# mLSTM denominators once per head and stream, and row scaling on ScalarE, in a two-layer encoder trunk

## The chip, the cores and the metric

The kernel runs on one core of a Trainium2 chip. The metric is the device time of one execution in microseconds, lower is better; the time of a kernel is the median of its runs. The engines are TensorE (PE; PEld is its weight load), VectorE (DVE), ScalarE (ACT), GpSimd (POOL) and SyncE (SP), which issues nearly all DMAs. Each engine runs its own instructions in order.

## The reference, cut to what matters

A hybrid encoder trunk of two layers (model width 1024) is applied to two request groups, a prompt of 256 tokens and a sample of 512 tokens. In each layer, eight grouped-query attention heads (C), four mLSTM heads (B) and four dilated attention heads (A) work on one projected input; cross-attention and a gated MLP follow. The mLSTM part, per head and chunk, in both directions:

```python
num = w_state[..., None] * jnp.einsum('nhld,nhde->nhle', qc, C) + jnp.einsum('nhls,nhse->nhle', w_intra, vc)
den = w_state * jnp.einsum('nhld,nhd->nhl', qc, n) + jnp.sum(w_intra, axis=-1)
h = num / jnp.maximum(jnp.abs(den), jnp.exp(-m_loc))[..., None]
...
hs = (hcat[:B] + flip(hcat[B:])).transpose(0, 2, 1, 3)
```

The forward and the backward scan each have their own denominator for each token; the two results are added.

## The kernel before, in words

The tokens of both groups stand side by side, 768 columns; `STREAMS` are (256, 512), the sample, and (0, 256), the prompt. The kernel does the mLSTM as masked attention over the whole stream. A query tile is 128 tokens, so a head has 4 tiles in the long stream and 2 in the short one, 6 per head, 24 per layer and 48 in all.

`attend` does one head and stream: for each query tile the scores (L375, L376, into one of two PSUM banks "S"), then `soft`, which turns scores into weights `p`; then the transposes of all tiles' weights (L387, into one of two banks "T"), a split into a high and a low half (ACT cast L183, DVE subtract L158), and the products with the values (L395, L396, into the single bank "Y").

For mLSTM heads `soft` is `b_soft`. For one tile it adds the triangular masks to the gate rows of the diagonal block (DVE, L158, with `cs`), takes Exps of the gate rows (ACT, L755 to L759: forward weights left of and on the diagonal, backward weights on and right of it), and multiplies them by the scores with a sum (DVE, L761, shown in the trace as CUSTOM_DVE_ANT_0 and a DVE_READ_ACCUMULATOR2): `p[:, 0:d1]` is the forward part with sum 0, `wb = gd[:, 1]` the backward diagonal block with sum 1, `p[:, d1:n]` the rest of the backward part with sum 2. L761 is the last reader of the scores, so it gives the bank "S" back. Then, per tile, four small DVE steps on the [128, 4] tile `dn` (add, absolute value, maximum with a column of `colm`, reciprocal), the row multiplies `smul("V", ...)` (L172, one on the forward part, and one on the backward rest if there is one), and a scalar_tensor_tensor (STT, L161) that adds the scaled backward diagonal block to `p`.

The weights and the gate tiles `gdt` lie in `arena_f`, of 13,824 fp32 columns, which is handed out by the `Arena` class in the order of the program text, oldest free place first. Gate rows come by DMA from `scr_g` (L725).

The order on each engine is set by a scheduler from priorities. `ahead(first, second)` gives `first` a lower priority, so that the projections of the next group of heads fill the gaps of the heads at hand: `b_proj(1)` beside `b_attn(0)` (heads 0 and 1), `a_proj(0)` beside `b_attn(1)` (heads 2 and 3). The heads themselves follow one another as the buffers permit.

Of the kernel before, what the change touches and what calls it, by code (L numbers as in the profile page):

```python
# [9 lines left out]
F32 = mybir.dt.float32  # L10
# [3 lines left out]
ALU = mybir.AluOpType  # L14
# [94 lines left out]
def trunk_kernel(ctx, tc, xT, memT, w_in, w_out, w_xq, w_xkv, w_xo, w_up, w_dn, w_dnt, par, fin_g, cst, fmk, tabs,  # L109
# [251 lines left out]
        for p0, src in pieces:  # L361
            SY.dma_start(out=dst.bitcast(F32)[p0:p0 + src.shape[0], :src.shape[1]], in_=src)

    def attend(qs, q0, nq, KH, KL, k0, nk, vv, vt0, e, y, y0, soft):
        n = nq * 128
        ni = 512 // nk
        ptiles, held = [], []
        for b in range(nq // ni):
            s = bank("S", "s").rearrange("p (i k) -> p i k", i=ni)
            pt = palloc()  # L370
            p = pt.rearrange("p (i k) -> p i k", i=ni)
            for j in range(ni):
                i = b * ni + j
                qa = qs[:, q0 + i * 128:q0 + (i + 1) * 128]
                PE.matmul(s[:, j], qa, KH[:, k0:k0 + nk], start=True, stop=False)  # L375
                PE.matmul(s[:, j], qa, KL[:, k0:k0 + nk], start=False, stop=True)  # L376
            soft(s, p, b * ni, ni)
            ptiles += [p[:, j] for j in range(ni)]
            held.append(pt)
        yps = bank("Y", "yps")  # L380
        nkt = nk // 128
        nb = 512 // n
        for kb in range(0, nkt, nb):
            t = bank("T", "t")
            for j in range(nb):
                for i in range(nq):
                    PE.transpose(t[:, j * n + i * 128:j * n + (i + 1) * 128],  # L387
                                 ptiles[i][:, (kb + j) * 128:(kb + j + 1) * 128], ident)
            ph, pl = asm.tile(512), asm.tile(512)
            hi_op(pick("ph_" + SITE[0], "A"), ph, t)  # L390
            tt(pl, t, ph.bitcast(F32), ALU.subtract)
            for j in range(nb):
                kt = kb + j
                w = vv[:, vt0 + kt]
                PE.matmul(yps[:, :n], w, ph[:, j * n:(j + 1) * n], start=kt == 0, stop=False)  # L395
                PE.matmul(yps[:, :n], w, pl[:, j * n:(j + 1) * n], start=False, stop=kt == nkt - 1)  # L396
            asm.free(ph, pl)
        af.free(*held)
        yo = y[64 * e:64 * e + 64, y0:y0 + n]
        hi_op(pick("yo_" + SITE[0], "A"), yo, yps[64 - 64 * e:128 - 64 * e, :n])  # L400
        tt(yo, yps[64 * e:64 * e + 64, :n], yo, ALU.add)
# [111 lines left out]
    def mixers(l, xt, x_dram, stats):  # L513
# [215 lines left out]
        def b_attn(pb, sv):  # L729
            SITE[0] = "b%d" % pb  # L730
            sts, vv, rows = sv
            for e in range(2):
                qs, K = sts[e]
                hd = 2 * pb + e
                for c0, n in STREAMS:
                    gb = rows[e][:, 2 * c0:2 * c0 + 2 * n].rearrange("p (d k) -> p d k", d=2)
                    attend(qs, c0, n // 128, K[:, :T], K[:, T:], c0, n, tok(vv[e]), c0 // 128, e, yt[5 + pb], c0,
                           b_soft(gb, c0, n, hd))
                af.free(rows[e])
                ar.free(qs, K, vv[e])  # L740

        def b_soft(gb, c0, n, hd):
            def soft(s, p, i0, ni):
                for j in range(ni):
                    one(s[:, j], p[:, j], i0 + j)

            def one(s, p, i):
                ti = c0 // 128 + i
                d0, d1 = i * 128, (i + 1) * 128
                nm = lambda d: colm[:, 2 * ti, d, hd:hd + 1]  # L750
                gdt = af.tile(256)
                gd = gdt.rearrange("p (d k) -> p d k", d=2)
                tt(gd, gb[:, :, d0:d1], tri, ALU.add)
                if i:
# [2 lines left out]
                A.activation(gd[:, 1], gd[:, 1], ACT.Exp, bias=nm(1))  # L757
                if d1 < n:
                    A.activation(p[:, d1:n], gb[:, 1, d1:n], ACT.Exp, bias=nm(1))  # L759
                dn = st.tile([128, 4], F32, tag="dn", name="dn")  # L760
                ttr = lambda o, s0, s1, c: V.tensor_tensor_reduce(  # L761
                    out=o, in0=s[:, s0:s1], in1=o, scale=0.125, scalar=0.0,
                    op0=ALU.mult, op1=ALU.add, accum_out=dn[:, c:c + 1])
                wb = gd[:, 1]
                ttr(p[:, 0:d1], 0, d1, 0)
                ttr(wb, d0, d1, 1)
                if d1 < n:
                    ttr(p[:, d1:n], d1, n, 2)
                    tt(dn[:, 1:2], dn[:, 1:2], dn[:, 2:3], ALU.add)
                stt(dn[:, 0:2], dn[:, 0:2], -1.0, dn[:, 0:2], ALU.mult, ALU.max)  # L770
                tt(dn[:, 0:2], dn[:, 0:2], colm[:, 2 * ti + 1, :, hd], ALU.max)
                V.reciprocal(dn[:, 0:2], dn[:, 0:2])
                smul("V", p[:, 0:d1], p[:, 0:d1], dn[:, 0:1])
                stt(p[:, d0:d1], wb, dn[:, 1:2], p[:, d0:d1], ALU.mult, ALU.add)
                if d1 < n:
                    smul("V", p[:, d1:n], p[:, d1:n], dn[:, 1:2])
                af.free(gdt)
            return soft

        def a_proj(pg):  # L780
            if pg == 0:
# [593 lines left out]
```

## Time and profile before

| What | Value |
|---|---|
| median of 3 runs | 2203.67 us (2197.82 to 2207.76) |
| profiled execution, its own time | 2199.17 us |
| its span from the first to the last instruction | 2197.3 us |
| mean granted TensorE clock | 0.952 of full speed |
| instructions | 31315 |

The span is the profiled execution from its first to its last instruction, on the one core. The busy share of an engine is an average over stages with different limits; what the mLSTM heads of the two layers cost is read from their own stretches, between about 250 and 345 us and between about 1328 and 1426 us.

### The profile page before, as it was taken

The page shows a single profiled execution, that of the slowest core. Times are in us where ns is not written, and L with a number is a line of the kernel's source. Part 1 is how long each engine was busy: PE and PEld are TensorE (multiplying, and loading weights), DVE is VectorE, ACT ScalarE, POOL GpSimd, SP SyncE. Part 2 cuts the span into 40 slices and gives each one's busy share as a digit, 9 for nine tenths or more (in the row PEclk, how much of TensorE's full clock was granted, in tenths as well). Part 3 has the DMA queues.
Part 4 walks back from the last instruction along what each step waited for, and adds up shares of the span by engine and source line. Part 5 has one row for each costly group of instructions (what it writes and reads, how often), then busy time and mean ns, then how long its engine had stood idle before and what let it go on. Part 6 is the DMA issues. An engine that isn't in the chain of part 4 may idle for free.

```text
span 2197.3 us, 31315 instructions
## 1 busy us (share of the span) xinstructions
PE 2032.2 (92%) x11256; PEld 1801.6 (82%) x11256; DVE 1924.4 (88%) x4191; ACT 1032.9 (47%) x2030; POOL 2.3 (0%) x28
## 2 busy tenths in 40 slices
PE   7989888998889999999999897899978999999996
PEld 5868677787779999999888685787868899999995
DVE  8777897877899999999978879888888999999997
ACT  4256645546533333333443666474654333333342
POOL 0000000000000000000000000000000000000000
PEclk8989989999899999999999898899988999999998
DMA  5523334343212222222234234344421222222211
GB/s 178 147 72 91 92 94 100 97 125 106 77 59 86 68 68 68 68 69 75 92 140 121 72 80 114 76 124 131 129 77 63 82 68 68 68 67 68 74 33 68
DMA packets 64684, 195.16 MB, mean 89 GB/s; under 512 B 8264, under 2 KB 11592, under 8 KB 63760
## 3 DMA queue, kind: packets, MB, share of 16 engines
q1 hardware_dynamic: 64528, 193.15, 30.1%
q8 instruction: 89, 1.46, 0.3%
q14 instruction: 67, 0.55, 0.1%
HBM read 150.17 MB, written 10.71 MB: 73 GB/s over the span
## 4 chain that ended last, share of the span: by engine, by line
PE 70%; DVE 21%; ACT 4%; DMA 3%; issue 2%; SPq 1%; DVEq 0%; ACTq 0%
PE rps L1075 8%; PE rps L1073 8%; PE rps L1074 8%; DVE arena_f L158 5%; PE rps L1116 5%; PE rps L1117 5%; PE rps L1118 5%; PE prS L213 4%; PE prS L214 4%; PE prS L215 4%; DVE arena_r L158 3%; DVE arena_f L161 2%; DVE xall L158 2%; PE t L387 2%; DVE wl L158 2%
## 5 line engine op out<-in xcount | busy, mean ns | idle before, releaser
L183 ACT CAST wh<-arena_f 128x512 fp32r<-128x512 f32 x280 | 170.6, 620 | 267.2 <-PE rps L1074 216.5
L183 ACT CAST wh<-wr 128x512 fp32r<-128x512 f32 x268 | 164.7, 620 | 264.4 <-PE rps L1074 101.8
L158 DVE TENSOR_TENSOR arena_f<-arena_f 128x512 f32<-128x512 f32 (+3 forms) x381 | 271.9, 732 | 16.3 <-DMA arena_f<-in_w_up 6.4
L158 DVE TENSOR_TENSOR wl<-wr,wh 128x512 fp32r<-128x512 f32 x288 | 197.1, 687 | 35.0 <-ACT wh L183 30.9
L1075 PE MATMUL rps<-xha,wl 128*128 128x384 f32 x640 | 212.1, 338 | 8.4 <-DVE wl L158 8.4
L1073 PE MATMUL rps<-xha,wh 128*128 128x384 f32 x640 | 216.3, 338 | 1.6 <-ACT wh L183 1.5
L1074 PE MATMUL rps<-xla,wh 128*128 128x384 f32 x640 | 216.0, 338 | 0.0
L158 DVE TENSOR_TENSOR xall<-rps,xall 128x256 f32<-128x256 f32 (+1 forms) x384 | 198.8, 554 | 15.9 <-PE rps L1196 5.1
L1116 PE MATMUL rps<-arena_r,wh 128*128 128x512 f32 (+1 forms) x608 | 202.6, 340 | 3.3 <-DVE xall L158 3.3
L1117 PE MATMUL rps<-arena_r,wh 128*128 128x512 f32 (+1 forms) x608 | 200.9, 338 | 0.5 <-DVE arena_r L158 0.4
L213 PE MATMUL prS<-xha,wh 128*128 128x512 f32 x480 | 193.6, 407 | 5.4 <-DVE arena_r L158 3.3
L215 PE MATMUL prS<-xha,wl 128*128 128x512 f32 x480 | 193.5, 404 | 3.3 <-DVE wl L158 3.1
L214 PE MATMUL prS<-xla,wh 128*128 128x512 f32 x480 | 193.0, 404 | 0.8 <-DVE xla L158 0.8
L158 DVE TENSOR_TENSOR wl<-arena_f,wh 128x512 fp32r<-128x512 f32 x280 | 189.6, 687 | 1.2 <-ACT wh L183 1.0
L158 DVE TENSOR_TENSOR arena_f<-rps,arena_f 128x384 f32<-128x384 f32 x280 | 151.9, 555 | 33.5 <-PE rps L1075 29.8
L1118 PE MATMUL rps<-arena_r,wl 128*128 128x512 f32 (+1 forms) x608 | 178.1, 338 | 0.0
L1073 PE MATMUL rps<-arena_r,wh 128*128 128x384 f32 x480 | 162.8, 340 | 1.3 <-ACT wh L183 1.3
L1074 PE MATMUL rps<-arena_r,wh 128*128 128x384 f32 x480 | 161.8, 337 | 0.0
L1075 PE MATMUL rps<-arena_r,wl 128*128 128x384 f32 x480 | 156.0, 339 | 0.6 <-DVE wl L158 0.5
L158 DVE TENSOR_TENSOR arena_r<-t,arena_r 128x512 fp32r<-128x512 f32 x184 | 125.1, 685 | 27.3 <-ACT arena_r L183 26.6
L213 PE MATMUL prP<-xha,wh 128*128 128x256 f32 x480 | 141.9, 296 | 7.0 <-DVE arena_f L158 3.4
L387 PE MATMUL t<-cs,arena_f 128*128 128x128 f32 x736 | 128.0, 291 | 13.6 <-DVE arena_r L158 8.3
(211 smaller groups left out, 4976.8 us busy)
## 6 DMA issues: line engine op xcount, KB each, us to landing
arena_f<-in_w_up SPq DMA_DIRECT2D x80, 512.0 KB
wr<-in_w_in SPq DMA_DIRECT2D x42, 512.0 KB
wr<-in_w_dn SPq DMA_DIRECT2D x40, 512.0 KB
wr<-in_w_out SPq DMA_DIRECT2D x32, 512.0 KB
arena_r<-arena_r SPq DMA_DIRECT2D x32, 384.0 KB
arena_r<-arena_r SPq DMA_DIRECT2D x48, 192.0 KB
xall<-in_xT SPq DMA_DIRECT2D x8, 768.0 KB
arena_r<-arena_r SPq DMA_DIRECT2D x64, 96.0 KB
```

Of the source, the lines that this page charges most:

```text
L158: V.tensor_tensor(out, a, b, op=op)
L183: A.copy(out, a)
L213: PE.matmul(ps, h[:, j], xh[i][:, c0:c0 + n], start=i == 0, stop=False)
L214: PE.matmul(ps, h[:, j], xl[i][:, c0:c0 + n], start=False, stop=False)
L215: PE.matmul(ps, lo[:, j], xh[i][:, c0:c0 + n], start=False, stop=i == tot - 1)
L387: PE.transpose(t[:, j * n + i * 128:j * n + (i + 1) * 128], ptiles[i][:, (kb + j) * 128:(kb + j + 1) * 128], ident)
L1073: PE.matmul(ps, h[:, k], x[k], start=k == 0, stop=False)
L1074: PE.matmul(ps, h[:, k], x[4 + k], start=False, stop=False)
L1075: PE.matmul(ps, lo[:, k], x[k], start=False, stop=k == 3)
L1116: PE.matmul(ps, h[:, m], hh[i][:, c], start=k == 0 and not tail, stop=False)
L1117: PE.matmul(ps, h[:, m], hlo[i][:, c], start=False, stop=False)
L1118: PE.matmul(ps, lo[:, m], hh[i][:, c], start=False, stop=i == b - 1)
```

## The change

The four small steps are no longer done per tile. `dn` becomes a [128, 4, 3] tile per head and stream (four buffers of the pool), the reductions of each tile write their row of it, and after the last tile of the stream a new function `settle_p` does the add, the absolute value, the maximum and the reciprocal once, on all tiles. It then scales the rows of each tile with `smul("A", ...)`, an ACT activation Copy with a scale from a column (L170), both parts of a tile, and adds the scaled backward diagonal block with the STT on DVE as before. The gate tiles are held until then. What is computed is the same.

```diff
-    def attend(qs, q0, nq, KH, KL, k0, nk, vv, vt0, e, y, y0, soft):
+    def attend(qs, q0, nq, KH, KL, k0, nk, vv, vt0, e, y, y0, soft, settle_p=None):
...
+        if settle_p:
+            settle_p(ptiles)
         yps = bank("Y", "yps")
...
         def b_soft(gb, c0, n, hd):
+            nq, t0 = n // 128, c0 // 128
+            dn = st.tile([128, 4, 3], F32, tag="dn", name="dn", bufs=4)
+            gds = []
...
-                dn = st.tile([128, 4], F32, tag="dn", name="dn")
                 ttr = lambda o, s0, s1, c: V.tensor_tensor_reduce(
                     out=o, in0=s[:, s0:s1], in1=o, scale=0.125, scalar=0.0,
-                    op0=ALU.mult, op1=ALU.add, accum_out=dn[:, c:c + 1])
-                wb = gd[:, 1]
+                    op0=ALU.mult, op1=ALU.add, accum_out=dn[:, i, c:c + 1])
                 ttr(p[:, 0:d1], 0, d1, 0)
-                ttr(wb, d0, d1, 1)
+                ttr(gd[:, 1], d0, d1, 1)
                 if d1 < n:
                     ttr(p[:, d1:n], d1, n, 2)
-                    tt(dn[:, 1:2], dn[:, 1:2], dn[:, 2:3], ALU.add)
-                stt(dn[:, 0:2], dn[:, 0:2], -1.0, dn[:, 0:2], ALU.mult, ALU.max)
-                tt(dn[:, 0:2], dn[:, 0:2], colm[:, 2 * ti + 1, :, hd], ALU.max)
-                V.reciprocal(dn[:, 0:2], dn[:, 0:2])
-                smul("V", p[:, 0:d1], p[:, 0:d1], dn[:, 0:1])
-                stt(p[:, d0:d1], wb, dn[:, 1:2], p[:, d0:d1], ALU.mult, ALU.add)
-                if d1 < n:
-                    smul("V", p[:, d1:n], p[:, d1:n], dn[:, 1:2])
-                af.free(gdt)
-            return soft
+
+            def settle_p(ps):
+                tt(dn[:, 0:nq - 1, 1], dn[:, 0:nq - 1, 1], dn[:, 0:nq - 1, 2], ALU.add)
+                d = dn[:, 0:nq, 0:2]
+                stt(d, d, -1.0, d, ALU.mult, ALU.max)
+                tt(d, d, colm[:, 2 * t0 + 1:2 * (t0 + nq):2, :, hd], ALU.max)
+                V.reciprocal(d, d)
+                for i, p in enumerate(ps):
+                    d0, d1 = i * 128, (i + 1) * 128
+                    smul("A", p[:, 0:d1], p[:, 0:d1], dn[:, i, 0:1])
+                    if d1 < n:
+                        smul("A", p[:, d1:n], p[:, d1:n], dn[:, i, 1:2])
+                    stt(p[:, d0:d1], gds[i][:, 128:256], dn[:, i, 1:2], p[:, d0:d1], ALU.mult, ALU.add)
+                af.free(*gds)
+            return soft, settle_p
```

The scheduler plans the order anew. The place shown is in the first layer, the end of head 0 (long and short stream); the names carry the numbers of their tiles. On DVE the order before is this: `dn_2413`, `dn_2431` and their like are tiles of single query tiles, L172 the row multiplies, L161 on `arena_f_76` the STTs.

```order
L172 TENSOR_SCALAR arena_f_76<-arena_f_76,dn_2431 128x512
L172 TENSOR_SCALAR arena_f_76<-arena_f_76,dn_2413 128x384
L172 TENSOR_SCALAR arena_f_76<-arena_f_76,dn_2413 128x128
L158 TENSOR_TENSOR xall_70<-yps_2118,xall_70 64x256
L161 SCALAR_TENSOR_TENSOR arena_f_76<-arena_f_76,dn_2394 128x128
L158 TENSOR_TENSOR dn_2569<-dn_2569 128x1
L161 SCALAR_TENSOR_TENSOR dn_2550<-dn_2550 128x2
L158 TENSOR_TENSOR dn_2531<-dn_2531,colm_466 128x2
L772 RECIPROCAL dn_2487<-dn_2487 128x2
L172 TENSOR_SCALAR arena_f_76<-arena_f_76,dn_2502 128x256
L161 SCALAR_TENSOR_TENSOR arena_f_76<-arena_f_76,dn_2431 128x128
```

In the change the same engine has this there; `dn_2368` is the tile of head 0's long stream, `dn_2464` that of its short stream, `dn_2506` that of head 1's long stream, and the additions with `cs_84` are masks for later tiles.

```order
L158 TENSOR_TENSOR dn_2464<-dn_2464,colm_466 128x2x2
L158 TENSOR_TENSOR xall_70<-yps_2118,xall_70 64x256
L161 SCALAR_TENSOR_TENSOR arena_f_76<-arena_f_76,dn_2368 128x128
L158 TENSOR_TENSOR dn_2506<-dn_2506 128x3
L779 RECIPROCAL dn_2464<-dn_2464 128x2x2
L158 TENSOR_TENSOR arena_f_76<-arena_f_76,cs_84 128x256 x2
L161 SCALAR_TENSOR_TENSOR arena_f_76<-arena_f_76,dn_2368 128x128
L158 TENSOR_TENSOR arena_f_76<-arena_f_76,cs_84 128x256 x4
L161 SCALAR_TENSOR_TENSOR arena_f_76<-arena_f_76,dn_2368 128x128
L158 TENSOR_TENSOR arena_r_77<-vps_2348,arena_r_77 128x4x64
L161 SCALAR_TENSOR_TENSOR arena_f_76<-arena_f_76,dn_2464 128x128 x2
```

The row multiplies and most small steps are gone from DVE; the four STTs of the long stream stand apart, with additions for later tiles between them. On ACT, at the same place, the order before is this: the copies are the results of the attention heads before (`yps_2068`, `yps_2118`), L347 is a cast of the next group's values, L756 and L757 are Exps of later tiles.

```order
L183 COPY xall_70<-yps_2068 64x512
L757 ACTIVATE arena_f_76<-arena_f_76,colm_466 128x128 x2
L183 COPY xall_70<-yps_2118 64x256
L347 CAST arena_r_77<-vps_2348 128x4x64
L183 CAST arena_r_77<-t_2440 128x512
L183 CAST arena_r_77<-t_2449 128x512
```

In the change ACT has this there, with L762 and L763 in the place of L756 and L757.

```order
L183 COPY xall_70<-yps_2118 64x256
L170 ACTIVATE arena_f_76<-arena_f_76,dn_2368 128x128
L170 ACTIVATE arena_f_76<-arena_f_76,dn_2368 128x384
L170 ACTIVATE arena_f_76<-arena_f_76,dn_2368 128x256 x2
L170 ACTIVATE arena_f_76<-arena_f_76,dn_2368 128x384
L170 ACTIVATE arena_f_76<-arena_f_76,dn_2368 128x128
L170 ACTIVATE arena_f_76<-arena_f_76,dn_2368 128x512
L347 CAST arena_r_77<-vps_2348 128x4x64
L170 ACTIVATE arena_f_76<-arena_f_76,dn_2464 128x128 x2
L170 ACTIVATE arena_f_76<-arena_f_76,dn_2464 128x256
L762 ACTIVATE arena_f_76<-arena_f_76,colm_466 128x128
L763 ACTIVATE arena_f_76<-arena_f_76,colm_466 128x128
```

The ten row multiplies of head 0 stand together, behind the copies, and the Exps of later tiles and the casts of transposed weights come after them.

## Rows read from the trace of the kernel before

**Rows 1.** The page's first part: busy us (share of the span) xinstructions
```profile
PE 2032.2 (92%) x11256; PEld 1801.6 (82%) x11256; DVE 1924.4 (88%) x4191; ACT 1032.9 (47%) x2030; POOL 2.3 (0%) x28
```

**Rows 2.** Busy time by stretch; columns as the first line says
```profile
core 0: us, PE busy (x) PEld busy (x) DVE busy (x) ACT busy (x) POOL busy (x), PEclk, DMA share, GB/s
252.00:288.00 36.00, 25.53 (x92) 17.05 (x91) 35.72 (x165) 23.59 (x63) 0.00 (x0) 0.72 0.38 97
288.00:316.00 28.00, 28.00 (x168) 25.16 (x167) 24.33 (x86) 10.87 (x23) 0.00 (x0) 0.94 0.18 49
316.00:344.00 28.00, 23.57 (x115) 18.18 (x114) 27.64 (x118) 16.81 (x41) 0.00 (x0) 0.88 0.41 100
1330.00:1366.00 36.00, 23.89 (x94) 16.28 (x93) 31.84 (x154) 20.23 (x54) 0.00 (x0) 0.77 0.44 107
1366.00:1398.00 32.00, 32.00 (x189) 28.08 (x190) 25.84 (x77) 13.28 (x28) 0.00 (x0) 0.99 0.27 81
1398.00:1426.00 28.00, 21.39 (x96) 16.13 (x95) 27.61 (x129) 15.54 (x37) 0.00 (x0) 0.76 0.44 104
```

**Rows 3.** Groups by form on DVE: count | busy us, mean ns | idle before
```profile
L161 DVE SCALAR_TENSOR_TENSOR arena_f<-arena_f,dn 128x128 f32<-128x128 f32 x48 | 16.2, 347 | 0.0
...
L172 DVE TENSOR_SCALAR arena_f<-arena_f,dn 128x128 f32<-128x128 f32 x32 | 8.3, 283 | 0.0
L172 DVE TENSOR_SCALAR arena_f<-arena_f,dn 128x256 f32<-128x256 f32 x24 | 7.5, 343 | 0.0
...
L172 DVE TENSOR_SCALAR arena_f<-arena_f,dn 128x384 f32<-128x384 f32 x16 | 6.6, 411 | 0.0
L158 DVE TENSOR_TENSOR dn<-dn 128x1 f32<-128x1 f32 x32 | 4.9, 155 | 0.1
L172 DVE TENSOR_SCALAR arena_f<-arena_f,dn 128x512 f32<-128x512 f32 x8 | 3.8, 476 | 0.0
```

**Rows 4.** The tile `dn`, who waited for it: us in total, times
```profile
  PE s L375: 22.4, 17
```

**Rows 5.** Timeline of DVE, around 271.6 us: start us, length us, instruction
```profile
271.60 0.15 DVE L158 TENSOR_TENSOR dn<-dn 128x1 f32<-128x1 f32 x1
271.67 0.15 DVE L161 SCALAR_TENSOR_TENSOR dn<-dn 128x2 f32<-128x2 f32 x1
271.74 0.15 DVE L158 TENSOR_TENSOR dn<-dn,colm 128x2 f32<-128x2 f32 x1
271.81 0.16 DVE L772 RECIPROCAL dn<-dn 128x2 f32<-128x2 f32 x1
```

**Rows 6.** Groups by form on ACT: count | busy us, mean ns | idle before
```profile
L185 ACT ACTIVATE xha<-xall,pr 128x512 fp32r<-128x512 f32 x42 | 29.1, 717 | 21.3 <-DVE xall L158 15.2 <-PE prS L215 5.9
...
L757 ACT ACTIVATE arena_f<-arena_f,colm 128x128 f32<-128x128 f32 x48 | 18.6, 393 | 4.3 <-DVE arena_f L158 4.3
...
L755 ACT ACTIVATE arena_f<-arena_f,colm 128x384 f32<-128x384 f32 x8 | 4.9, 611 | 1.6 <-DVE arena_f L158 1.1 <-PE t L387 0.5
...
L755 ACT ACTIVATE arena_f<-arena_f,colm 128x256 f32<-128x256 f32 x8 | 4.0, 500 | 3.4 <-DVE arena_f L158 3.4
```

**Rows 7.** Timeline of ACT, around 264 us
```profile
263.63 0.41 ACT L756 ACTIVATE arena_f<-arena_f,colm 128x128 f32<-128x128 f32 x1
263.92 0.41 ACT L757 ACTIVATE arena_f<-arena_f,colm 128x128 f32<-128x128 f32 x1
264.21 0.41 ACT L756 ACTIVATE arena_f<-arena_f,colm 128x128 f32<-128x128 f32 x1
```

**Rows 8.** Busy time by stretch, the two parts of the first one
```profile
252.00:264.00 12.00, 9.14 (x40) 6.00 (x38) 11.91 (x47) 11.84 (x32) 0.00 (x0) 0.86 0.21 50
264.00:288.00 24.00, 16.39 (x52) 11.05 (x53) 23.81 (x119) 11.75 (x33) 0.00 (x0) 0.65 0.47 121
```

**Rows 9.** Waits of ACT in 1326 to 1436 us: total, times, longest
```profile
ACT arena_f L755 <- DMA arena_f<-scr_g: 7.1, 1, 7.1
```

**Rows 10.** The chain that ended last, same stretch: start us, length us
```profile
1344.29 7.73 DMA arena_f<-scr_g
```

More of the change, by code (lines that the diff above doesn't have):

```diff
@@ L737, in b_attn @@
                     attend(qs, c0, n // 128, K[:, :T], K[:, T:], c0, n, tok(vv[e]), c0 // 128, e, yt[5 + pb], c0,
-                           b_soft(gb, c0, n, hd))
+                           *b_soft(gb, c0, n, hd))
                 af.free(rows[e])
@@ L747, in one @@
             def one(s, p, i):
-                ti = c0 // 128 + i
                 d0, d1 = i * 128, (i + 1) * 128
-                nm = lambda d: colm[:, 2 * ti, d, hd:hd + 1]
+                nm = lambda d: colm[:, 2 * (t0 + i), d, hd:hd + 1]
                 gdt = af.tile(256)
+                gds.append(gdt)
                 gd = gdt.rearrange("p (d k) -> p d k", d=2)
```

## The prediction

> **What bounds the kernel now.** I began with the page's first part, which gives each engine's busy time. TensorE is busy for 92% of the 2197.3 us span and VectorE (DVE) for 88%, while ScalarE (ACT) is busy for 47% [rows 1]. The average says that TensorE is the bound, but the change touches only the mLSTM heads, so the second view was busy time by stretch. It shows four stretches in which DVE is the full engine and TensorE is not: 252 to 288 and 1330 to 1366 us (the first two heads of each layer), 316 to 344 and 1398 to 1426 us (the other two) [rows 2]. DVE is busy 35.72 of 36 us, 27.64 of 28, 31.84 of 36 and 27.61 of 28. TensorE is idle for 10.5, 4.4, 12.1 and 6.6 us of them, 33.6 us in all, and its mean granted clock is 0.72 to 0.88. In the stretches between (288 to 316, 1366 to 1398) TensorE is busy throughout with projections. So time can be had only inside the four stretches, and the idle 33.6 us is about as much as there is, if the clock stays as it is.
>
> The third view, everything that touches the denominator tile `dn`, says who waits: the score matmuls on TensorE (L375) waited 17 times, 22.4 us together, for DVE work on `dn`, that is for the two score banks that the reductions of L761 give back [rows 4]. DVE's pace frees the banks; TensorE follows.
>
> **What the change removes from DVE.** Two kinds of work leave. First the 80 row multiplies of L172, which go to ACT. Their mean durations at 128, 256, 384 and 512 columns are 283, 343, 411 and 476 ns, times 32, 24, 16 and 8: 26.2 us [rows 3]. Second the four small steps (add, abs, max, reciprocal). They are 32 + 48 + 48 + 48 = 176 instructions, and become 16 of each, one set per head and stream (four heads, two streams, two layers): 64, so 112 fewer. Each lasts 0.15 to 0.16 us, but in the timeline they start 0.07 us apart (271.60, 271.67, 271.74, 271.81) [rows 5]: on a full engine only the distance of starts counts. 112 x 0.07 = 7.8 us. The same overlap of 0.08 us, taken off each of the 80 multiplies, leaves 26.2 - 6.4 = 19.8 us. DVE is relieved of 27.6 us, 6.9 us per stretch. The upper bound, with full durations, is 26.2 + 112 x 0.155 = 43.6 us; I take 27.6, because the engine is full where it counts. The 64 new small ones work on at most 8 columns instead of 2, which I price at nothing.
>
> The product with the second diagonal block (48 STTs) stays on DVE and still comes after the multiplies, now one engine further.
>
> **What it adds to ACT.** 80 ACTIVATEs with a scale from a [128,1] column. The trace has no such Copy; the nearest rows are the Exps of the same stage, fp32 from and to the same arena with a bias from a column: 393 ns at 128 columns, 500 at 256, 611 at 384, and the scaled Identity at 512, 717 ns [rows 6]. Sum: 12.6 + 12.0 + 9.8 + 5.7 = 40.1 us. Back to back the Exps start 0.29 us apart at 0.41 us length [rows 7], so 0.12 us each overlap, and ACT's time is 40.1 - 9.6 = 30.5 us, 7.6 us per stretch. Per 512-token head and stream there are seven of them, 2 x 0.28 + 2 x 0.38 + 2 x 0.49 + 0.60 = 2.9 us; per 256-token one three, 0.9 us.
>
> Is there room on ACT? It is busy 23.59, 16.81, 20.23 and 15.54 us of the four stretches [rows 2]. But not evenly: in 252 to 264 it is full (11.84 of 12), from 264 to 288 it works 11.75 of 24 [rows 8]. The multiplies come after the reductions, so they fall mostly into the second part. With 7.6 us more, ACT would need 31.2, 24.4, 27.8 and 23.1 us; DVE, less 6.9, needs 28.8, 20.7, 24.9 and 20.7. In each stretch **ACT takes DVE's place as the fuller engine**. A stretch can shrink to ACT's need at best: by 4.8, 3.6, 8.2 and 4.9 us. The 8.2 us of the third is doubtful: there ACT stands for 7.1 us in front of an Exp (L755) whose gate rows come by DMA from `scr_g`, and the chain of work that ended last goes through that transfer for 7.73 us from 1344.29 [rows 9, 10]. A faster DVE doesn't fetch those rows earlier unless the load's issue moves too; if all of the wait stays, 1.1 us is left there. I take 4. Sum of the best case per stretch: 4.8 + 3.6 + 4 + 4.9 = 17.3 us.
>
> **What the new order costs.** The order of instructions shows that the multiplies of a head and stream stand as one block on ACT: seven, a cast, then three, in a row, behind the copies of two other results, and the Exps of later tiles stand behind the block. On DVE the STTs of the block stand one by one among additions for later tiles, so DVE, which runs its queue in order, waits at each STT for ACT's two multiplies. Behind those STTs are the reductions that free the score banks. Before, the multiplies of a tile were on the same engine as the STT and there was no such handover. There are 16 blocks, and in none can I expect both engines to stay full. A loss of all 17.3 us is the lower bound of what is gained, none lost the upper one; nothing in the trace is nearer to one end, so I take half: **a gain of 9 us**.
>
> The chain from the last reduction to the transposes grows as well. Before, for a 512-token stream, it was four small steps (0.3 us), a multiply 0.48 and an STT 0.35: 1.1 us. Now it is 0.3 + 2.9 + 0.35 = 3.5 us, so 2.4 more; for 256 tokens about 0.6 more. 8 x 3.0 = 24 us in all. I cost it at nothing beyond the half above, because the work that hides it is the next head's scores, Exps and reductions, whose inputs don't depend on this head; if that cover is gone, it costs up to 24 us.
>
> Held longer are the 256-column gate tiles: four of them, 1024 columns, per 512-token stream on top of 2048 for the products, of an arena of 13,824. It reuses the oldest free place, so I cost this at nothing; two such streams fit. No DMA is added. In layer 1 the 512-column gate load of the third head now stands ahead of the 256-column one of the fourth; that is part of the 4 us.
>
> Sum against the profiled execution: 2199.2 - 9 = 2190.2 us. The median of the runs shown, 2203.67, is 0.2% above that execution; carried over, the forecast is **2195 us**, own range 2189 to 2201.
>
> **The rivals.**
> *ACT keeps up.* Its idle half (264 to 288, and the 288 to 316 stretch, where it works 10.87 of 28 us [rows 2]) takes multiplies and early Exps, so that DVE's relief counts in full: 27.6 us less about 5 for the DMA wait, 22 us: 2177 on the profiled footing, 2182 us. For it speaks that TensorE's waits name DVE; against it, ACT's full first part and the sums above. Chance 0.27.
> *Nothing comes of it.* The handover eats the whole gain, or the projections behind the stretches take it up: 2204 us. For it: the stretches of the second pair of heads hold projections. Against it: the first pair has none in 252 to 288. Chance 0.15.
> *ScalarE's block takes the path: slower.* If the 24 us of longer chains show through instead of lying beside the next head's work, and the relief counts only by 9, the time rises by 15 us: 2214, or 2219 us. It decides from 9 of the 24 us upwards, about three eighths. For it: the Exps that the next reductions need are behind the block on ACT. Against: two score banks and three heads' tiles are in flight. Chance 0.18. The Trainium skill, "ScalarE: Activation LUTs", section Rules for kernel authors, would have it so: for add and mul it says to use VectorE, not ScalarE. The trace agrees on the price of one (476 ns against 717 ns at 512 columns [rows 3, 6]), and leaves open whether ACT's idle time pays it.
>
> **How the numbers follow.** Forecast 0.40, the rivals 0.27, 0.15 and 0.18. A measurement of this kernel can tell about 0.5%, 11 us, from no change. Faster by more than that: the first rival and a quarter of the forecast's chance, with a little off, 0.38. Slower: nearly all of the last rival, 0.17. Within: 0.45. The range goes from a little under the first rival, 2178, to just short of the last, 2216.
>
> **What would show each step.** In the profile after: DVE's busy time lower by 26 to 44 us, ACT's higher by 30 to 40; an ACTIVATE Copy of 0.38 to 0.42 us at 128 columns; the four stretches shorter by 2 us each, with ACT busier than DVE in them; STTs on `dn` that wait for ACT, where none had any idle time before it [rows 3]; fewer waits of L375 for DVE. The forecast is wrong if the stretches shrink by 6 us or more each, with DVE still full (the first rival), or grow, with TensorE idle in front of transposes that wait for ACT's multiplies (the last). The planned order also differs outside the mLSTM stages; a difference of some us there, with no mLSTM wait in it, would be none of these.

## The result and the profile after

| Kernel | Median | Lowest to highest |
|---|---|---|
| before (same rounds) | 2202.74 us | 2197.82 to 2207.76 |
| changed | 2179.74 us | 2174.64 to 2181.64 |

The ratio is 0.9892, 95% interval 0.9864 to 0.992: faster by 23 us, where 9 were forecast. (A ratio compares runs of the same rounds; it is not the quotient of two medians of a table.) The profiled execution of the changed kernel took 2181.64 us, its span is 2179.5 us, 17.8 less than before. The spans differ by less than the medians because the profiled execution lies 3.6 us below the median before and 1.9 above it after.

The page's first part, to be held against [rows 1]:

```profile
PE 2016.9 (93%) x11256; PEld 1791.4 (82%) x11256; DVE 1898.8 (87%) x3999; ACT 1061.3 (49%) x2110; POOL 2.3 (0%) x28
```

DVE lost 25.6 us of busy time and 192 instructions (80 multiplies, 112 small steps), ACT gained 28.4 us and 80 instructions. The groups by form, first on ACT, then on DVE (count | busy us, mean ns | idle before), answer to [rows 3, 6]:

```profile
L170 ACT ACTIVATE arena_f<-arena_f,dn 128x128 f32<-128x128 f32 x32 | 11.9, 398 | 2.4 <-DVE dn L779 2.3
L170 ACT ACTIVATE arena_f<-arena_f,dn 128x256 f32<-128x256 f32 x24 | 11.2, 501 | 0.0
L170 ACT ACTIVATE arena_f<-arena_f,dn 128x384 f32<-128x384 f32 x16 | 9.7, 605 | 0.0
L170 ACT ACTIVATE arena_f<-arena_f,dn 128x512 f32<-128x512 f32 x8 | 5.7, 713 | 0.0
```

```profile
L161 DVE SCALAR_TENSOR_TENSOR arena_f<-arena_f,dn 128x128 f32<-128x128 f32 x48 | 16.0, 347 | 3.8 <-ACT arena_f L170 3.5
```

The multiplies cost what the Exps had promised: 398, 501, 605 and 713 ns against 393, 500, 611 and 717. The handover cost little: the STTs waited for ACT for 3.5 us in all. The tile `dn` says the same; its first line here is idle time of DVE, the second who waited for `dn`, where [rows 4] had 22.4 us:

```profile
  ACT arena_f L170: 3.5, 9
...
  PE s L375: 18.1, 20
```

Busy time by stretch, with the columns of [rows 2]. The stretches lie 2 us later in the first layer and 14 to 20 us earlier in the second, and some are cut to another length, so the share of a stretch is what to compare:

```profile
254.00:284.00 30.00, 20.52 (x83) 14.04 (x84) 26.99 (x114) 25.62 (x69) 0.00 (x0) 0.84 0.35 78
284.00:312.00 28.00, 26.73 (x163) 23.23 (x163) 20.32 (x50) 15.93 (x36) 0.00 (x0) 0.99 0.28 87
312.00:340.00 28.00, 22.90 (x118) 18.21 (x117) 27.45 (x112) 22.14 (x58) 0.00 (x0) 0.88 0.44 104
1316.00:1346.00 30.00, 20.02 (x89) 13.04 (x87) 24.85 (x100) 21.09 (x55) 0.00 (x0) 0.83 0.48 113
1346.00:1378.00 32.00, 29.43 (x171) 25.17 (x172) 22.41 (x62) 20.00 (x49) 0.00 (x0) 0.94 0.27 80
1378.00:1410.00 32.00, 27.01 (x127) 21.34 (x126) 28.94 (x114) 23.27 (x60) 0.00 (x0) 0.84 0.39 91
```

DVE is no longer full in the first stretch (26.99 of 30 us) and still full in the third row (27.45 of 28). ACT comes near it, but is behind DVE in each of them.

How long the mLSTM heads of a layer take is read from the reductions, L761 before and L766 after: count, duration in ns (min/median/max), then the start of the first and of the last. Kernel before, first and second layer:

```profile
L761 DVE DVE_READ_ACCUMULATOR2_ANT dn<- x64: 73/89/105, 252.5 to 336.4; 128x1 f32 x64
...
L761 DVE DVE_READ_ACCUMULATOR2_ANT dn<- x64: 74/83/98, 1332.5 to 1417.5; 128x1 f32 x64
```

The changed kernel:

```profile
L766 DVE DVE_READ_ACCUMULATOR2_ANT dn<- x64: 72/83/89, 255.1 to 332.1; 128x1 f32 x64
...
L766 DVE DVE_READ_ACCUMULATOR2_ANT dn<- x64: 72/82/85, 1316.7 to 1400.2; 128x1 f32 x64
```

The first layer's heads went from 83.9 to 77.0 us, the second layer's from 85.0 to 83.5. That is 8.4 us of a span that fell by 17.8. The first and last starts of other lines say where the rest lies. The attention heads (A) of the first layer, from the last reduction to the last mask step (L437 before), went from 70.6 to 62.4 us. The two feed-forward stages, first to last up matmul, went from 916.8 to 912.0 us together. The feed-forward stages hold no instruction that the change touches. The stretch of the A heads begins with the scaling of the last mLSTM head, whose last STT ends 12.1 us after the last reduction before (348.5) and 5.5 us after it in the changed kernel (337.6); the rest of it holds none.

So there were three theories, which do not exclude each other. *The change itself*: the scaling, the denominators worked out once, or both, relieve DVE. *The queue*: the new plan puts the last K stacks of the first layer's A heads ahead of the stored memory's loads on SP. *The placement*: the tile `dn` had twelve buffers, each padded to 32 bytes of a partition, and has four of 64, so both arenas lie 128 bytes lower in SBUF (in the built program `arena_f` starts at byte 106,720 before and at 106,592 after).

### The profile page after: what moved, and what is told of

It is laid out like the page before. It is cut to its first block, busy times and chain, and to the rows that moved or that the text cites. A ratio compares the mean times of both kernels' runs of the same rounds, so it can differ in the third digit from the quotient of the medians.

```text
span 2179.5 us, 31203 instructions
## 1 busy us (share of the span) xinstructions
PE 2016.9 (93%) x11256; PEld 1791.4 (82%) x11256; DVE 1898.8 (87%) x3999; ACT 1061.3 (49%) x2110; POOL 2.3 (0%) x28
## 4 chain that ended last, share of the span: by engine, by line
PE 73%; DVE 17%; ACT 5%; DMA 2%; issue 2%; SPq 0%; DVEq 0%; ACTq 0%
PE rps L1084 8%; PE rps L1082 8%; PE rps L1083 8%; PE rps L1125 5%; PE rps L1126 5%; PE rps L1127 5%; PE prS L213 5%; DVE arena_f L158 4%; PE prS L214 4%; PE prS L215 4%; PE t L389 2%; PE prP L213 2%; PE prP L214 2%; DVE wl L158 2%; PE prP L215 2%
## 5 line engine op out<-in xcount | busy, mean ns | idle before, releaser
L215 PE MATMUL prP<-xha,wl 128*128 128x256 f32 x480 | 139.3, 290 | 0.5 <-DVE wl L158 0.5
```

The source lines that it names most:

```text
L215: PE.matmul(ps, lo[:, j], xh[i][:, c0:c0 + n], start=False, stop=i == tot - 1)
```

## The experiments

All ratios are to the kernel before, run in the same rounds. Stretches are from the profiled execution, in us: mLSTM heads of the first layer, A heads of the first layer (both as above), the two feed-forward stages, mLSTM heads of the second layer (the expectations count mLSTM heads from the multiply ahead of the first read, 0.2 us more). The feed-forward column compares where what goes before it is alike; e8 and e12 do not fit into it. Pairs that differ in the 128 or 256 bytes alone have the same order of work on every engine in the built programs. e4 differs from the changed kernel in SP's order alone. Every other edit made the scheduler plan the order anew, on TensorE and DVE too (e12's in the second layer alone), so its price holds that other order as well. Kernels that are a line longer above a place show its line number one higher.

| Kernel | Median us | Ratio (95%) | mLSTM 1 | A 1 | Feed-forward | mLSTM 2 |
|---|---|---|---|---|---|---|
| before | 2202.74 | 1 | 83.9 | 70.6 | 916.8 | 85.0 |
| changed | 2179.74 | 0.9892 (0.9864 to 0.992) | 77.0 | 62.4 | 912.0 | 83.5 |
| e1 before, loads late | 2195.67 | 0.9979 (0.997 to 0.9988) | 84.0 | 61.1 | 919.1 | 83.2 |
| e2 once, scaling on DVE | 2181.7 | 0.9918 (0.9903 to 0.9932) | 82.1 | 61.3 | 910.5 | 82.5 |
| e3 per tile, scaling on ACT | 2188.83 | 0.9953 (0.994 to 0.9965) | 77.2 | 62.6 | 918.8 | 84.3 |
| e4 changed, two writes ahead | 2176.04 | 0.9897 (0.988 to 0.9913) | 77.0 | 63.8 | 913.7 | 83.2 |
| e5 before, 128 bytes on | 2194.22 | 0.9961 (0.9946 to 0.9975) | 84.2 | 69.6 | 911.0 | 84.5 |
| e6 changed, 128 bytes on | 2183.56 | 0.9914 (0.9898 to 0.993) | 77.0 | 62.8 | 917.6 | 83.5 |
| e7 e1 and 128 bytes on | 2186.78 | 0.9934 (0.992 to 0.9947) | 84.2 | 61.4 | 913.7 | 82.2 |
| e8 changed, gate rows early | 2203.0 | 1.0004 (0.9995 to 1.0012) | 85.0 | 70.1 | 904.2 | 87.6 |
| e9 before, 256 bytes on | 2201.23 | 0.9998 (0.9988 to 1.0009) | 84.0 | 70.3 | 918.2 | 85.6 |
| e10 e3 and 128 bytes on | 2181.97 | 0.991 (0.9897 to 0.9922) | 77.3 | 62.2 | 914.8 | 83.3 |
| e11 changed, four writes ahead | 2180.46 | 0.9898 (0.9883 to 0.9912) | 77.2 | 70.1 | 910.2 | 80.0 |
| e12 changed, gate rows early in layer 2 | 2186.26 | 0.9927 (0.9915 to 0.994) | 77.1 | 61.1 | 916.3 | 87.9 |

### The parts of the change: e2 and e3

```diff
 # e2, from the changed kernel
-                    smul("A", p[:, 0:d1], p[:, 0:d1], dn[:, i, 0:1])
+                    smul("V", p[:, 0:d1], p[:, 0:d1], dn[:, i, 0:1])
 # e3, from the kernel before
-                smul("V", p[:, 0:d1], p[:, 0:d1], dn[:, 0:1])
+                smul("A", p[:, 0:d1], p[:, 0:d1], dn[:, 0:1])
 # in both the second part of a row likewise
```

> The changed kernel with the row multiplies back on VectorE: denominators once per head and stream, nothing moved to ScalarE. Its DMA queue has the key stacks ahead of the memory loads, as the changed kernel. Theory A: VectorE is relieved of 7.8 us of 27.6, so 2 us of the mLSTM stretches, and the 8 us of the DMA wait: about 10 us faster than before, 8 us slower than the changed kernel. Theory B: 7.8 of 27.6 of the gain, about 6 us faster than before, 17 slower than the changed kernel.

> The kernel before with the row multiplies on ScalarE, tile by tile, and the small steps per tile as they were. Its DMA queue too has the key stacks ahead of the memory loads. Theory A: relief of 19.8 us of 27.6, no block of multiplies, so 5 us of the mLSTM stretches and 8 us of the DMA wait: about 13 us faster than before. Theory B: 19.8 of 27.6 of the gain, about 16 us faster. If the blocks of multiplies cost the changed kernel much, this one is as fast as it or faster.

The scaling on ACT alone gives the whole gain of the first layer's mLSTM heads (77.2 us); the denominators once, with the scaling left on DVE, give 1.8 us. In total e3 came nearest to its first theory (10 us, 13 expected); e2 gained 18 us, and both its theories (10 and 6) missed, since neither had a term for the placement. But both runs have A heads of 61 to 63 us, and e2 has the short feed-forward stages, e3 the long ones. Their times can't be read as prices of the two parts before these are separated.

### The queue: e1, e4 and e11

e1 holds the loads of the stored memory back until a K stack of the A heads has landed; e4 puts two, e11 four writes of 512 KB ahead of those stacks in the changed kernel.

```diff
 # e1, from the kernel before (K likewise)
+        G.tensor_copy(late, sa1[0][1][1].bitcast(F32)[:, 0:1])
...
             vt = rtl(1024)
+            G.tensor_copy(vt[:, 0:1], late)
             SY.dma_start(out=vt.bitcast(F32), in_=scr_v[l, j])
 # e4, from the changed kernel; e11 has range(4) and parts[j % 2]
+                if l == 0:
+                    for j in range(2):
+                        SY.dma_start(out=scr_z[j], in_=parts[j].bitcast(F32)[:, 0:1024])
             sts = stacks(*parts)
```

> The kernel before, with one thing changed: the loads of the cross-attention memory (scr_v, scr_k) wait, through a one-column copy on GpSimd, until the last key stacks of the dilated heads have landed, so they stand behind those stacks in the DMA queue as they do in the changed kernel. Theory A (about half of the gain is a by-effect of the new order: in the first layer the 11.2 us wait of a score matmul for its key stacks goes away): 6 to 10 us faster than before, about 0.4%, with nothing changed in the mLSTM heads, and that wait gone or down to 3 us. Theory B (all of the gain is VectorE's relief; the shorter stage behind the mLSTM heads is work that was drawn forward): within 2 us of before.

> The changed kernel with the suspected cost put back: in the first layer two extra transfers of 512 KB each from SBUF to a scratch tensor stand in the queue ahead of the last key stacks of the dilated heads, as the memory loads did before. Theory A: 4 to 8 us slower than the changed kernel, with a wait of score matmuls for the stacks of some 5 us or more. Theory B: within 2 us of the changed kernel.

> The changed kernel with four extra writes of 512 KB to memory (two of each half of the K parts) queued ahead of the last K stacks of the first layer's attention; two such writes cost nothing that showed. The order of everything else stays. Theory of the stacks: in the kernel before the loads of 512 KB and more ahead of these stacks, and their issue at 370 instead of 364 us, held the score matmuls for 11 us; with four writes ahead the stacks come 5 to 9 us later, the score matmul at the start of the A heads waits for DMA 4 to 9 us, and 3 to 8 us of time are lost (2183 to 2188 us). Rival: the gain in the A heads had another cause (the order of matmuls there); a wait for the stacks shows and the time stays within 2 us of the changed kernel.

SP's queue, in the kernel before and then in the changed one (start us, length us); L362 with `arena_r<-arena_r` are the K stacks, `scr_v` and `scr_k` the stored memory:

```profile
368.65 1.11 SPq L912 DMA_DIRECT2D arena_r<-scr_v  x1
369.85 0.47 SPq L362 DMA_DIRECT2D arena_r<-scr_k  x1
370.41 5.46 SPq L362 DMA_DIRECT2D arena_r<-arena_r  x6
```

```profile
363.70 8.41 SPq L362 DMA_DIRECT2D arena_r<-arena_r  x4
372.21 0.52 SPq L921 DMA_DIRECT2D arena_r<-scr_v  x1
```

The chain of work that ended last, kernel before, at the start of the A heads (start us, length us), and busy time of 378 to 386 there:

```profile
372.47 11.20 DMA arena_r<-arena_r
383.68 0.04 issue
383.72 0.80 PE s L375
```

```profile
378.00:386.00 8.00, 3.93 (x12) 2.87 (x12) 1.81 (x3) 1.45 (x3) 0.00 (x0) 0.64 1.03 222
```

No engine is busy for more than half of these 8 us while the DMA engines are full (share 1.03). The 11.20 us are the transfer's own time, not a wait of the score matmuls, as two expectations have it: TensorE waits 1.3 us for it at L375, and a cast on ACT (L347) 3.8 us, behind which TensorE waits 3.4 us for ACT, 4.7 us together. In e1 the same piece of the chain is 5.65 us, from 370.64 on, TensorE waits 2.1 us for it, and the A heads last 61.1 us. The kernel gained 5 us, where 6 to 10 or under 2 had been expected. In the changed kernel no such wait is left. e4, the clean test, shows no cost in time: the score matmuls waited 2.3 us for the stacks, and the A heads last 1.4 us longer. e11 brought the wait back (chain, then waits: us in total, times, longest):

```profile
372.28 5.73 DMA arena_r<-arena_r
378.14 0.76 PE s L376
```

```profile
PE s L376 <- DMA arena_r<-arena_r: 4.9, 1, 4.9
```

Its A heads last 70.1 us, 7.7 more than in the changed kernel, which agrees with stacks that set that stretch. But its total did not rise. It is 5.8 us behind the changed kernel at the second layer's first reduction (1322.3 against 1316.5), 2.2 at the last one, and level at the second layer's first up matmul (1669.7 in both). The expectation that the order of everything else stays did not hold: in the built program TensorE's order differs from its 1717th matmul on, and DVE's and ACT's orders differ too. So e11 doesn't price the wait, and what gave the time back isn't shown. Taken out of the kernel before, the wait was worth 0.21% (e1), and 0.27% on top of the moved arenas (e5 to e7), each with the new order that came with the edit; put into the changed kernel, nothing.

### The placement: e5, e6, e7, e9

```diff
-        rcm = st.tile([128, 4], F32, tag="rcm", name="rcm", bufs=1)
+        rcm = st.tile([128, 36], F32, tag="rcm", name="rcm", bufs=1)[:, 0:4]
 # 36 columns: 128 bytes (e5, e6, e7, e10); e9 has 68 columns: 256 bytes
```

> Kernel before with nothing but a wider small table (32 more f32 columns), so that every buffer behind it, the two arenas among them, lies 128 bytes further on in SBUF; the instructions and their order stay. The changed kernel's arenas lie 128 bytes from where the kernel before had them, because its denominators' tiles are padded less. Theory of the layout: the two feed-forward stages (from the first to the last up matmul, 916.8 us together in before, 912.0 in after) get 5 to 7 us shorter, and the kernel takes 2192 to 2197 us. Rival, that the layout does nothing and the feed-forward stages differ by what goes before them: both stages within 1.5 us of before, and a time within 2 us of before in the same rounds.

> The changed kernel with its small table 32 f32 columns wider, so that its arenas lie where those of the kernel before lie; instructions and order as in the changed kernel. Theory of the layout: the feed-forward stages go from 912 back to about 917 to 919 us, the time rises by 5 to 7 us to about 2185 to 2187 us (ratio to before 0.993). Rival, layout does nothing: 2178 to 2182 us, ratio 0.989 to 0.991.

> Kernel before with none of the change, but with the two side effects of it put in by hand: the loads of the stored memory wait for the last K stacks of the first layer's attention, and the arenas lie 128 bytes further on. If the two side effects add up: the loads alone gave 5 us, the layout another 5 to 7, so 2188 to 2191 us (ratio 0.993 to 0.995). Rival, layout does nothing: as with the late loads alone, ratio 0.997 to 0.999, about 2195 to 2197 us.

> Control to the run with the arenas 128 bytes further on: the kernel before with its small table 64 f32 columns wider, so that the buffers behind it lie 256 bytes further on. Instructions and order as before. Theory: what counts is where the arenas lie within steps of 256 bytes, so nothing changes: 572 matmuls in each 100 us from 1800 to 2100 (577 with 128 bytes), and a ratio of 0.998 to 1.002. Rival: any move of the arenas away from where they lay helps; then 577 again and a ratio near 0.996.

Busy time of 100 us in the second layer's feed-forward, where TensorE never waits and its granted clock is 1.00 (2.4 GHz); what counts is the number of matmuls behind PE. In this order: before, e5, e9, changed, e6.

```profile
1900.00:2000.00 100.00, 100.00 (x573) 95.43 (x572) 94.66 (x160) 37.91 (x58) 0.00 (x0) 1.00 0.23 69
```

```profile
1900.00:2000.00 100.00, 100.00 (x577) 95.80 (x576) 94.75 (x161) 37.75 (x58) 0.00 (x0) 1.00 0.22 66
```

```profile
1900.00:2000.00 100.00, 100.00 (x574) 95.44 (x573) 94.67 (x161) 37.82 (x58) 0.00 (x0) 1.00 0.23 69
```

```profile
1900.00:2000.00 100.00, 100.00 (x576) 95.08 (x576) 95.86 (x163) 36.40 (x55) 0.00 (x0) 1.00 0.22 69
```

```profile
1900.00:2000.00 100.00, 100.00 (x572) 95.16 (x571) 94.76 (x160) 35.89 (x55) 0.00 (x0) 1.00 0.23 69
```

Same instructions in the same order, and 0.7% more matmuls when the arenas lie 128 bytes from where they lay; 256 bytes change nothing. In all 14 kernels the count in the stretches 1800 to 1900, 1900 to 2000 and 2000 to 2100 goes with the placement, whatever else was changed: 570 to 574 in the five with the arenas as before or 256 bytes on, 575 to 578 in the nine with the other one. Three pairs differ in the placement alone: the second layer's feed-forward goes from 454.0 to 450.7 (before, e5), from 454.3 to 451.0 (e1, e7), and from 450.3 to 453.7 us back (changed, e6); the first layer's by 2.1 to 2.5 us. The groups by form, 1700 to 2130 us, before and then e5 (columns as in [rows 3]):

```profile
L1073 PE MATMUL rps<-arena_r,wh 128*128 128x384 f32 x221 | 75.0, 339 | 0.5 <-ACT wh L183 0.5
```

```profile
L1073 PE MATMUL rps<-arena_r,wh 128*128 128x384 f32 x228 | 76.4, 335 | 0.5 <-ACT wh L183 0.5
```

The up matmuls that stream from the arena are 3 to 4 ns shorter each; those that stream from `xha` and `xla`, which did not move, 1 to 2 ns (338 to 336 or 337), and the down matmuls (512 columns) 0 to 2. In whole-kernel time the 128 bytes are worth 0.39% (e5), 0.45% (e1 to e7), 0.43% (e3 to e10), and 0.22% on the way back (changed to e6). In that last pair the intervals of the times overlap, and it is the stage that tells (912.0 to 917.6). The feed-forward stages hold 5.8 of the 8.6 us of e5; where the rest lies was not looked at. In e5 the small tables behind the padded one move too, in the changed kernel `colm` and the first `dn` do not; the count of matmuls goes with the arenas in both, and in e6. The layout's theory was met by e5, e7 and e9, and in e6 by the stage, while its time rose by less than the 5 to 7 us expected.

### The change without its side effects: e10 against e7

> Kernel before with its row scaling on ScalarE, the denominators still worked out per query tile, and the arenas 128 bytes further on. It has the scaling half of the change and both side effects, so against the late loads with moved arenas (2186.8 us, neither half of the change) it shows the scaling alone, and against the changed kernel the denominators worked out once. If the terms add up: 0.9953 less 0.004 for the layout, 0.991 to 0.992, 2183 to 2185 us. Rival, that the parts do not add (the layout helps only where VectorE is the fuller engine): 0.994 to 0.996, no better than without the move.

e7 has the moved arenas and late memory loads, and nothing of the change; TensorE still waits 2.2 us for the stacks there. e10 has both side effects too, with the scaling on ACT, and no such wait. The reductions of the first layer, e7 and then e10:

```profile
L762 DVE DVE_READ_ACCUMULATOR2_ANT dn<- x64: 75/82/93, 252.0 to 336.2; 128x1 f32 x64
```

```profile
L761 DVE DVE_READ_ACCUMULATOR2_ANT dn<- x64: 74/81/86, 252.4 to 329.7; 128x1 f32 x64
```

The parts add up, as the first theory had it (2181.97 us, 2183 to 2185 expected). That gives a ladder with one edit at each step (and from the second step on a new order), in parts of 2203 us:

| Step | Ratio | Worth |
|---|---|---|
| before to e5, placement | 1 to 0.9961 | 8.6 us |
| e5 to e7, memory loads late | 0.9961 to 0.9934 | 5.9 us |
| e7 to e10, scaling on ACT | 0.9934 to 0.991 | 5.3 us |
| e10 to changed, denominators once | 0.991 to 0.9892 | 4.0 us |

Each ratio is good to about 0.0015, 3 us. The scaling has two more pairs, 0.9979 to 0.9953 (e1 to e3) and 0.9918 to 0.9892 (e2 to changed), 5.7 us each. The intervals of e10 and of the changed kernel overlap, so the last step is not told from nothing by this pair alone; e7 to e2, the other pair, gives 3.5 us, and its intervals overlap too. The stretches say little for it. They hold projections, which a new order can move out (TensorE has 323 matmuls in the first layer's mLSTM stretch before, 302 in the changed kernel), so the fair measure is from the first reduction to the end of the A heads. In the first layer that is 145.6 us in e7, 139.5 in e10 and 139.4 in the changed kernel: 6.1 us for the scaling, 0.1 for the denominators once. With the scaling on DVE the denominators are worth 2.2 us there (143.4 in e2). Of the last step's 4.0 us, 2.8 lie in the feed-forward stages, which the denominators don't touch. The scaling is shown, by e1 to e3 clear of the intervals; that the denominators once are worth 4 us is not.

### The second layer: e8 and e12

The changed kernel with the loads of the gates' rows written ahead of the stacks (e8 in both layers, e12 in the second):

```diff
-            sts = stacks(*parts)
-            vv = v_proj(10 + pb)
             rows = []
             for e in range(2):
...
                 rows.append(gbt)
+            sts = stacks(*parts)
+            vv = v_proj(10 + pb)
```

> The changed kernel with the loads of the gates' rows queued ahead of the second set of stacks. In the second layer VectorE waits 6.5 us for such a row at L761 in the changed kernel, and the stretch of that layer's b-heads got only 1.5 us shorter by the change, against 6.8 in the first layer. Theory: the row's arrival holds the second layer, so without the wait that stretch (83.7 us) falls by 3 to 6 us and the kernel takes 2174 to 2178 us. Rival, that what is late behind the row (VectorE's own work, the matmuls' operands) sets the stretch: the wait goes, the stretch stays within 1.5 us, the time within 2 us of after. The loads of the memory also come ahead of the last stacks of the first layer's A heads here; if that stops the score matmuls as it did before, 5 to 8 us are lost there.

> The changed kernel with the loads of the gates' rows queued ahead of the second set of stacks in the second layer alone; up to there every order is that of the changed kernel. Theory: the 6.5 us wait for such a row at L761 is why the second layer gained nothing; the stretch from the first to the last reduction there goes from 83.7 us to 78 to 80, and the time to 2174 to 2177 us. Rival, which the run with rows early in both layers speaks for (the wait went, the stretch grew to 87.8 us): another transfer or VectorE sets the end there, the stretch stays at 82 us or more and the time is no better than 2178 us.

The wait at L761 in the changed kernel is one of ACT, not of VectorE as two expectations have it: 6.5 us of ACT, and 3.3 us of DVE at its mask additions. In e8 the first is 0.2 us and in e12 it is gone, but DVE's is 5.0 us in both, and the stretch grew, from 83.5 to 87.6 and 87.9 us. e8's theory and e12's first one missed. e12's rival has the numbers right (82 us or more, no better than 2178 us), but its reason isn't shown, since a row still stands in the chain. The chain of the changed kernel and then of e12:

```profile
1331.30 0.32 PE yps L398
1331.61 0.33 SPq L727
1332.03 6.65 DMA arena_f<-scr_g
```

```profile
1328.25 0.44 PE t L389 x4
1328.72 9.78 DMA arena_f<-scr_g
```

The row's transfer follows TensorE's work in the chain in both kernels, and then takes 6.65 or 9.78 us. Written earlier in the program it does not start earlier: 15.3 us after the stretch's first reduction in the changed kernel, 15.5 in e12. That the row holds the second layer is therefore neither shown nor excluded. e8 is worth its run for another reason: the plan put the memory's loads ahead of the stacks again, as before the change, and the chain has this:

```profile
375.96 14.15 DMA arena_r<-arena_r
390.10 1.66 issue
391.76 0.77 PE s L375
```

ACT waits 7.9 us for the stacks at L347 there. With that, a gate row for which DVE waits 5.0 us in the first layer, 85.0 us for that layer's mLSTM heads and 87.6 for the second's, the whole gain of 23 us is gone, though every part of the change is in it and the arenas lie well.

## Why the prediction was right and wrong

**The time** lies in the wide range (2178 to 2216), below the forecast's own (2189 to 2201), and near the number of the first rival (2182), but not by its way: that it lands there is luck. On the ladder the change itself is worth 9.3 us, 5.3 for the scaling and 4.0 for the denominators, of which only the first is shown; that the sum is so near the 9 forecast is luck too. 14.5 us came from two side effects for which the sum had no term. These prices are counted up from the kernel before. Taken back singly from the changed kernel, the side effects cost less: 4.8 us for the placement (e6) and nothing for two writes ahead of the stacks (e4), so how much of the 14.5 us belongs to which is not closed.

**The step that failed** is the one from the stretches to the total, "time can be had only inside the four stretches". The prediction looked at DVE's and ACT's orders, held that "no DMA is added", and had no term for the new shape of the tile `dn`. Nothing was added, but SP's queue was planned anew, and a [128, 4, 3] tile in four buffers moved everything behind it. Its last sentence had kept a place for "a difference of some us there, with no mLSTM wait in it"; it was more than the change's own part.

**Prices.** The ACT price was right to 2% at each width. The expected changes of busy time were a little high: DVE -25.6 us where 27.6 stood in the sum, ACT +28.4 for 30.5. One sum slipped: the four durations times their counts give 27.7 us, not 26.2; 26.2 is the busy time of [rows 3], where overlap is already out. So the overlap was in part taken off twice, and put right the sum would have said 29.1 us.

**"ACT takes DVE's place as the fuller engine"** did not come true: DVE stays ahead in all stretches shown. The block of multiplies lay in ACT's idle time; the STTs waited 3.5 us for it, not half of 17.3. In the first layer's mLSTM heads the gain was 6.9 us, where half of 4.8 + 3.6 had been expected. That is most of what the ACT limit left, and half of the 13.8 us that the first rival's full relief would have given there. The condition "if the clock stays as it is" did not hold: TensorE's granted clock over that stretch, from first to last reduction, was 0.82 before and 0.89 in the changed kernel. It isn't needed for the gain: e3 has the same 77.2 us at 0.82.

**The second layer** had been given half of 4 + 4.9. It got 1.5 us in the mLSTM heads, and its A heads took 4.1 us longer (61.8 to 65.9), so nothing. They are as long in e1 (65.6), which has nothing of the change. The doubt about the gate row [rows 9, 10] was well placed: the transfer's part of the chain went from 7.73 to 6.65 us, ACT's wait for it from 7.1 to 6.5. Whether it is the cause is open.

**The longer chain** was mis-sized. The four small steps were put at 0.3 us. DVE's timeline at the end of head 2's long stream:

```profile
318.18 0.16 DVE L158 TENSOR_TENSOR dn<-dn 128x3 f32<-128x3 f32 x1
...
321.58 0.16 DVE L161 SCALAR_TENSOR_TENSOR dn<-dn 128x8 f32<-128x8 f32 x1
...
324.19 0.17 DVE L158 TENSOR_TENSOR dn<-dn,colm 128x8 f32<-128x8 f32 x1
...
325.35 0.19 DVE L779 RECIPROCAL dn<-dn 128x8 f32<-128x8 f32 x1
```

and ACT's, where ten multiplies follow in one block:

```profile
326.24 4.08 ACT L170 ACTIVATE arena_f<-arena_f,dn 128x128 f32<-128x128 f32 x10
```

From the first step to the reciprocal's end pass 7.4 us, since other work of a full DVE (27.45 of 28 us) stands between the steps; the block then takes 4.1 us for both streams, near the 3.8 of the sum. The chain is thus 7 us longer than costed at this place, and still hidden: in the whole kernel the transposes waited 2.2 us for the multiplies (L170), where they had waited 3.2 for L172 before. The last rival's cover held.

**The rule against the change.** The Trainium skill, "ScalarE: Activation LUTs", section Rules for kernel authors, says to use VectorE for mul. Three pairs of kernels keep it and break it: e2 and changed, e1 and e3, e7 and e10. Breaking it is 0.24 to 0.26% faster, clear of the intervals in e1 to e3. One multiply is dearer on ACT in this trace (713 ns at 512 columns against 476 [rows 3]), but ACT had idle time beside a full DVE. By the rule the time would have been that of e2, 2181.7 us.

No kernel of these runs is faster than the changed one by more than the intervals.

## What to carry to other kernels

Before a gain is put down to the work that an edit moves, set DMA queues and buffer addresses of both kernels side by side; a change of a tile's shape moves every buffer behind it, and a new plan reorders loads in stages that the edit never names. Pad a small tile as a control: it costs one line and shows what placement alone does. A ladder of kernels is only as clean as the orders that come with its steps: compare them too. In this kernel, moving a multiply to an engine where it takes longer paid, since that engine was idle beside a full one, even though the result had to come back.

## What the runs showed of the hardware

In this kernel the place of the arenas changes the rate of matmuls that wait for nothing: 572 or 577 in 100 us at full clock, by 128 bytes, and back by 256. Measured from `xall`, which is placed ahead of the padded table, the arenas start at an odd multiple of 128 bytes in the slow kernels and at a multiple of 256 in the fast ones (106,720 - 26,464 = 313.5 x 256 before; 106,592 - 26,464 = 313 x 256 after). The same holds measured from the buffers `wr` and `wh`; which pair of buffers matters, and by what mechanism, is open. The bare address doesn't decide: in e1 the arenas start at 106,752 = 417 x 256 and the stage is slow, in e7 at 106,880 = 417.5 x 256, and it is fast.

That speaks against the alignment of transfers as the cause. The Trainium skill, "DMA: Bandwidth & Descriptors", section How a descriptor splits into AXI transactions, says that a transaction must start at an address aligned to 256 bytes, so that a descriptor which starts elsewhere pays for bytes it doesn't use. If transfers to and from the arenas set the rate, e1 should by it be the faster of the two; the trace does not agree.
